# One section for the four column-group products of a modulation step, and one tile for its weights

## The chip, the core and the metric

The program runs on one NeuronCore of a Trainium2 chip. The metric is the device time of one execution in microseconds. TensorE (PE; its weight loads are shown as PEld) multiplies, VectorE (DVE), ScalarE (ACT) and GpSimd (POOL) work element by element, and SyncE (SP) issues the transfers between HBM and the core's SBUF. Products land in PSUM, eight banks of 512 f32 a partition.

## What is computed

Two networks run one after the other over 256 tokens of width 1024. The first is a hybrid block (attention, a delta rule, an MLP) and a recurrent block with an MLP. The second is a two-layer block of a diffusion kind, whose every normalisation is shifted, scaled and gated by a modulation vector that depends on two conditioning vectors only, `c` and `c_ctx`:

```python
def modulation(cvec, w_mod, b_mod):
    m = jax.nn.silu(cvec) @ w_mod + b_mod
    return jnp.split(m[:, None, :], N_MOD, axis=-1)
...
ml = modulation(c, w_mod[i], b_mod[i])
mc = modulation(c_ctx[None, :], w_mod[i], b_mod[i])
hl = modulate(rmsnorm(xl, g_pre_mix[i]), ml[0], ml[1])
```

`w_mod[i]` is 1024 x 6144 f32, 25 MB a layer. As it depends on nothing else, this product may be made at any time before the second network needs it.

## The kernel before

The large products of the kernel are f32 split in two: each weight half is copied by ScalarE to a rounded part (`wh`, line 404) and VectorE takes the rest (`wl`, line 405), six of each in rotation (`NW = 6`); three raw halves (`wr`, `NR = 3`) are loaded ahead by SyncE (line 386). Three matmuls, high by high, high by low and low by high, make one product. They go through the helper at line 343, as all matmuls do; transposes go through line 367.

The modulation is different: plain f32, in 48 steps. A step is one of 2 layers, one of 3 pairs of the six vectors, and one of 8 slices of the inner dimension. Its stationary operand is 32 columns wide (`cs_t`, both conditioning vectors and zeros), and its 2048 output columns are four groups of 512, which land in the partitions 0 to 31, 32 to 63, 64 to 95 and 96 to 127 of one PSUM bank, `pm`. So a step is four matmuls on four different column groups of the array (lines 772 to 774), and eight steps accumulate into the bank before VectorE takes it out (line 780).

The weights of a step are 1 MB. `mod_load` (line 726) loads them as two tiles of 512 KB (`wm`, four buffers), products 0 and 1 from the first and 2 and 3 from the second. SyncE issues them from the same queue as the weights of the large products. The generator `mods` keeps two steps loaded ahead.

The program is put in order by a planner that takes instructions by priority as they become ready. The generator is advanced by `fill(n)` from many places: 18 steps woven into the delta rule of the first network, the others between MLP units and at the borders of stages. Each of the four matmuls stands under `tc.high_priority(-10)`, which puts it ten places later in priority than its place in the program, so each may be moved by itself behind other work of TensorE.

Of the kernel before, what the change touches and what calls it, by code (L numbers as in the profile page):

```python
# [10 lines left out]
F32 = mybir.dt.float32  # L11
# [4 lines left out]
P = 128  # L16
# [15 lines left out]
def _unit(w, k0, nk, cols):  # L32

    n = w.shape[1]
    a = w.reshape(-1, P, n)[k0 : k0 + nk][:, :, cols]
    return a.transpose(1, 0, 2).reshape(P, -1)
# [83 lines left out]
def _ncols(c):  # L120
    return c.stop - c.start if isinstance(c, slice) else len(c)
# [5 lines left out]
def _cols(t):  # L127

    parts, at = [], 0

    def add(name, a):
        nonlocal at
        a = a.reshape(P, -1)
        COLS[name] = (at, a.shape[1])
        at += a.shape[1]
        parts.append(a)

    def vec(v):
        return v.reshape(-1, P).T

    def taps(w):
        return w.reshape(w.shape[0], -1, P).transpose(2, 1, 0)

    add("hyb_conv", taps(t("hyb_conv_w")[0]))
    add("norm_w", vec(t("hyb_norm_w")[0]))
    add("rec_conv", taps(t("rec_conv_w")[0]))
    add("rec_conv_b", vec(t("rec_conv_b")[0]))
    add("rec_b_a", vec(t("rec_b_a")[0]))
    add("rec_b_x", vec(t("rec_b_x")[0]))
    add("lam", vec(t("rec_lambda")[0]))  # L150
    for i in range(2):
        add(f"g_q{i}", vec(t("g_q_2")[i]))
        add(f"g_kv{i}", vec(t("g_kv_2")[i]))
        add(f"conf_w{i}", taps(t("conf_dw_w_2")[i]))
        add(f"conf_b{i}", vec(t("conf_dw_b_2")[i]))
        add(f"sc_w{i}", taps(t("sc_dw_w_2")[i]))
    return np.concatenate(parts, axis=1)
# [5 lines left out]
def _rows(t):  # L163
    r = []
    for i in range(2):
        for a in (1, 2):
            for b in "gb":
                r.append(t(f"ln{a}_{b}")[i])
    for i in range(2):
        r.append(t("g_branch_2")[i])  # L170
    for i in range(2):
        r.append(np.concatenate([t("conf_ln_g_2")[i], t("conf_ln_b_2")[i], np.zeros(512, np.float32)]))
    r.append(
        np.concatenate(
            [t("hyb_sinks")[0][HEAD_ORDER], t("hyb_a_log")[0], t("hyb_dt_bias")[0], np.zeros(1008, np.float32)]
        )
    )
    return np.stack(r)
# [50 lines left out]
def _pack(inputs):  # L229
    def t(name):  # L230
        return np.asarray(inputs[name])

    units = _weight_units(t)
    sizes = [(nk * _ncols(c), nk) for _, _, nk, c in units]
    wp = np.zeros((len(units), P, 2048), np.float32)
    for n, un in enumerate(units):
        a = _unit(*un)
        wp[n, :, : a.shape[1]] = a
    wm = np.ascontiguousarray(
        t("w_mod_2").reshape(2, 8, P, 3, 2, 1024).transpose(0, 3, 1, 4, 2, 5)  # L240
    )
    one = np.ones(1024, np.float32)
    bg = []
    for i in range(2):
        b = t("b_mod_2")[i].reshape(12, 512)
        g = np.concatenate(
            [one, t("g_pre_mix_2")[i], t("g_post_mix_2")[i], one, t("g_pre_mlp_2")[i], t("g_post_mlp_2")[i]]
        ).reshape(12, 512)
        bg.append(np.stack([b, g], 1).reshape(3, 4, 1024))
    cc = np.zeros((P, 8, 32), np.float32)  # L250
    cc[:, :, 0] = t("c_2")[0].reshape(8, P).T
    cc[:, :, 1] = t("c_ctx_2").reshape(8, P).T
    x = t("x")[0]
    kc0, kc1 = _consts()
    arrays = {
        "x": np.ascontiguousarray(x.reshape(2, P, 1024)),
        "xT": np.ascontiguousarray(x.T.reshape(8, P, 256).transpose(1, 0, 2)),
        "ctx": np.ascontiguousarray(t("ctx_2")[0].reshape(2, P, 1024)),
        "wp": wp,
        "wm": wm,  # L260
        "bg": np.ascontiguousarray(np.stack(bg)),
        "cc": cc,
        "cols": np.ascontiguousarray(_cols(t)),
        "rows": _rows(t),
        "kc": kc0,
        "kch": kc1,
    }
    return arrays, sizes
# [26 lines left out]
def hybrid_then_mla(ctx: ExitStack, tc: tile.TileContext, a, out, usizes):  # L295
    nc = tc.nc
    V, S, G, T = nc.vector, nc.scalar, nc.gpsimd, nc.tensor
    cpool = ctx.enter_context(tc.tile_pool(name="cpool", bufs=1))
    wpool = ctx.enter_context(tc.tile_pool(name="wpool", bufs=1))
# [8 lines left out]
    def nm(s):  # L308
        uid[0] += 1
        return f"{s}_{uid[0]}"  # L310
# [4 lines left out]
    def s4(shape, dt=F32):  # L315
        return tmp.tile(shape, dt, tag="s4", bufs=5, name=nm("s4"))

    def s2(shape, dt=F32):
        return tmp.tile(shape, dt, tag="s2", bufs=9, name=nm("s2"))
# [13 lines left out]
    def psC():  # L333
        return psp.tile([P, 512], F32, tag="pc", bufs=1, name=nm("pc"))

    def psM():
        return psp.tile([P, 512], F32, tag="pm", bufs=1, name=nm("pm"))
# [4 lines left out]
    def mm(o, l, r, start, stop):  # L342
        T.matmul(o, l, r, start=start, stop=stop)  # L343
# [12 lines left out]
    def K(name):  # L356
        w, o, n = KC[name]
        return kcs[w][:, o : o + n]
# [7 lines left out]
    def tr(o, i):  # L366
        T.transpose(o, i, ident)  # L367
# [345 lines left out]
    cs_t = cpool.tile([P, 8, 32], F32, name="cs_t")  # L713
# [9 lines left out]
    class WM:  # L723
        tiles, n = {}, 0

    def mod_load():

        if WM.n >= 48:
            return
        i, q, k = WM.n // 24, WM.n // 8 % 3, WM.n % 8  # L730
        for j in range(2):
            wm = wpool.tile([P, 2, 512], F32, tag="wm", bufs=4, name=nm("wm"))
            if WM.n < 2:
                G.tensor_copy(wm[:, 0, 0:1], WM.after)
            nc.sync.dma_start(out=wm, in_=a["wm"][i, q, k, j].rearrange("p (a b) -> p a b", a=2))
            WM.tiles[WM.n, j] = wm
        WM.n += 1

    mc = cpool.tile([P, 2, 3, 32], F32, name="mc")
# [7 lines left out]
    def mods():  # L747

        def cols_of(m, i, q):
            pt = psC()  # L750
            for c in range(4):
                tr(pt[:, 128 * c : 128 * c + 128], m[:, 128 * c : 128 * c + 128])
            V.tensor_copy(mc[:, i, q].rearrange("p (c r s) -> p c r s", c=4, r=4),
                          pt.rearrange("p (c r s) -> p c r s", c=4, r=4)[:, :, :, 0:2])

        todo = None
        for n in range(48):
            i, q, k = n // 24, n // 8 % 3, n % 8
            if k == 0:
                ps = psM()  # L760
            if k == 1 and todo:
                cols_of(*todo)
            if k == 4:
                bg = s4([P, 2, 512])
                for r in range(4):
                    nc.sync.dma_start(
                        out=bg[32 * r : 32 * r + 32],
                        in_=a["bg"][i, q, r : r + 1].rearrange("o (a b) -> o a b", a=2).to_broadcast([32, 2, 512]),
                    )
            while WM.n < min(n + 2, 48):  # L770
                mod_load()
            for r in range(4):
                with tc.high_priority(-10):
                    mm(ps[32 * r : 32 * r + 32, :], cs_t[:, k, :], WM.tiles[n, r // 2][:, r % 2, :], k == 0, k == 7)
            mod_load()
            if k < 7:
                yield
                continue
            m = s2([P, 512])
            V.tensor_tensor(m, ps, bg[:, 0, :], op=ADD)  # L780
            V.scalar_tensor_tensor(m, m, K("one")[:, q : q + 1], bg[:, 1, :], op0=ADD, op1=MUL)
            for r in range(4):
                if 2 * q + r // 2 in (2, 5):
                    nc.sync.dma_start(
                        out=mdr[i, :, 2 * q + r // 2, 512 * (r % 2) : 512 * (r % 2) + 512], in_=m[32 * r : 32 * r + 2]
                    )
            todo = (m, i, q)
            yield
        cols_of(*todo)
        yield  # L790

    mod_g = mods()

    def fill(n):
# [1268 lines left out]
```

## Time and profile before

| | |
|---|---|
| median of three runs | 1644.76 us (1640.21 to 1647.02) |
| the profiled execution, whole | 1647.52 us |
| span of its profile | 1645.5 us |
| TensorE busy | 1592.7 us, 97% |
| VectorE, ScalarE, GpSimd busy | 1032.0, 745.0, 95.6 us |
| transfers | 259.80 MB, 47.8% of 16 DMA engines' span |

Times in the rows are microseconds from the start of the span. "Busy" is the union of an engine's instructions; matmuls overlap, and the ends of their records are modelled. The chain that ended last is followed back from the last instruction, at each step to what released it.

### The profile page before, as it was taken

The page shows a single profiled execution, that of the slowest core. Times are in us where ns is not written, and L with a number is a line of the kernel's source. Part 1 is how long each engine was busy: PE and PEld are TensorE (multiplying, and loading weights), DVE is VectorE, ACT ScalarE, POOL GpSimd, SP SyncE. Part 2 cuts the span into 40 slices and gives each one's busy share as a digit, 9 for nine tenths or more (in the row PEclk, how much of TensorE's full clock was granted, in tenths as well). Part 3 has the DMA queues.
Part 4 walks back from the last instruction along what each step waited for, and adds up shares of the span by engine and source line. Part 5 has one row for each costly group of instructions (what it writes and reads, how often), then busy time and mean ns, then how long its engine had stood idle before and what let it go on. Part 6 is the DMA issues. An engine that isn't in the chain of part 4 may idle for free.

```text
span 1645.5 us, 25334 instructions
## 1 busy us (share of the span) xinstructions
PE 1592.7 (97%) x10182; PEld 1363.7 (83%) x10182; DVE 1032.0 (63%) x1593; ACT 745.0 (45%) x1264; POOL 95.6 (6%) x121
## 2 busy tenths in 40 slices
PE   8989999999989999998999999999999999989998
PEld 7856688887878998986877889999999878779997
DVE  6875475556787556777974753444444879765554
ACT  5642244443574445436344543322222565454443
POOL 0012000000000000003010100000000120000000
PEclk9999999999999999999999999999999999989999
DMA  8765576665658655443330343223223353146553
GB/s 281 254 235 187 180 225 221 207 199 180 212 181 291 209 192 175 165 166 103 118 101 26 129 141 103 90 90 103 92 88 103 118 184 96 58 133 204 181 192 103
DMA packets 72869, 259.80 MB, mean 158 GB/s; under 512 B 8480, under 2 KB 8736, under 8 KB 72752
## 3 DMA queue, kind: packets, MB, share of 16 engines
q1 hardware_dynamic: 72752, 258.19, 47.8%
q8 instruction: 80, 1.31, 0.3%
q14 instruction: 37, 0.30, 0.1%
HBM read 257.08 MB, written 1.08 MB: 157 GB/s over the span
## 4 chain that ended last, share of the span: by engine, by line
PE 81%; DVE 7%; ACT 3%; POOL 1%; issue 1%; DMA 1%; POOLq 0%; DVEq 0%; ACTq 0%; SPq 0%
PE pa L343 45%; PE pb L343 27%; PE pm L343 5%; PE pb L367 3%; DVE wl L405 1%; PE pc L367 1%; ACT s L1385 1%; POOL ti L1391 1%; DMA wr<-in_wp_dram 1%; DVE s L1579 1%; ACT wh L404 1%; DVE s L643 0%; DVE s L1404 0%; DVE b L709 0%; DVE b L647 0%
## 5 line engine op out<-in xcount | busy, mean ns | idle before, releaser
L405 DVE TENSOR_TENSOR wl<-wr,wh 128x1024 fp32r<-128x1024 f32 (+2 forms) x366 | 444.1, 1218 | 313.3 <-ACT wh L404 300.0
L404 ACT CAST wh<-wr 128x1024 fp32r<-128x1024 f32 (+2 forms) x364 | 377.2, 1042 | 451.2 <-PE pa L343 200.2
L343 PE MATMUL pa<-wh,b 128*128 128x512 f32 (+3 forms) x1456 | 409.9, 363 | 11.1 <-ACT b L646 5.6
L343 PE MATMUL pb<-b,wh 128*128 128x256 f32 x2240 | 406.6, 284 | 0.0
L343 PEld LDWEIGHTS pb<-b,wh 128*128 128x128 f32 x2240 | 352.8, 192 | 8.0 <-issue 3.4
L343 PE MATMUL pb<-b,wl 128*128 128x256 f32 x1120 | 317.7, 284 | 0.0
L343 PEld LDWEIGHTS pa<-wh,b 128*128 128x128 f32 x1456 | 266.1, 194 | 57.8 <-ACT b L646 6.1
L343 PE MATMUL pa<-wl,b 128*128 128x512 f32 (+3 forms) x728 | 257.2, 362 | 1.1 <-DVE wl L405 1.1
L343 PE MATMUL pa<-wh,s 128*128 128x512 f32 x768 | 244.5, 391 | 0.0
L343 PEld LDWEIGHTS pb<-b,wl 128*128 128x128 f32 x1120 | 215.0, 192 | 3.4 <-issue 3.4
L343 PE MATMUL pa<-b,wh 128*128 128x256 f32 x1056 | 198.7, 289 | 1.1 <-ACT b L646 0.8
L343 PEld LDWEIGHTS pa<-b,wh 128*128 128x128 f32 x1056 | 166.6, 193 | 14.2 <-issue 4.2
L343 PEld LDWEIGHTS pa<-wh,s 128*128 128x128 f32 x768 | 144.3, 188 | 29.3 <-DVE s L453 0.3
L343 PEld LDWEIGHTS pa<-wl,b 128*128 128x128 f32 x728 | 141.7, 195 | 24.6 <-issue 5.0
L343 PE MATMUL pa<-b,wl 128*128 128x256 f32 x528 | 149.9, 286 | 0.8 <-DVE wl L405 0.8
L343 PE MATMUL pa<-wl,s 128*128 128x512 f32 x384 | 150.1, 391 | 0.0
L343 PEld LDWEIGHTS pa<-b,wl 128*128 128x128 f32 x528 | 101.8, 193 | 2.9 <-issue 1.9
L343 PE MATMUL pm<-wm,cs_t 128*32 128x512 f32 x384 | 96.5, 618 | 4.7 <-DMA wm<-in_wm_dram 4.7
L343 PEld LDWEIGHTS pa<-wl,s 128*128 128x128 f32 x384 | 72.3, 188 | 13.4
L558 DVE TENSOR_TENSOR s<-s 128x512 f32<-128x512 f32 x80 | 54.9, 686 | 42.2 <-ACT s L556 42.2
L367 PE MATMUL pb<-kc_sb,s 128*128 128x128 f32 x366 | 59.9, 288 | 13.2 <-POOL s L1482 6.4
L1579 DVE SCALAR_TENSOR_TENSOR s<-cu,cols_sb,s 128x512 f32<-128x512 f32 (+1 forms) x120 | 71.7, 628 | 0.3
(278 smaller groups left out, 1405.8 us busy)
## 6 DMA issues: line engine op xcount, KB each, us to landing
wr<-in_wp_dram SPq DMA_DIRECT2D x354, 512.0 KB, 4.4
wm<-in_wm_dram SPq DMA_DIRECT2D x96, 512.0 KB, 4.7
row<-in_rows_dram SPq DMA_DIRECT2D x10, 512.0 KB, 5.4
wr<-in_wp_dram SPq DMA_DIRECT2D x8, 416.0 KB, 4.8
s<-in_bg_dram SPq DMA_DIRECT2D x24, 128.0 KB, 7.0
row<-mdr SPq DMA_DIRECT2D x6, 512.0 KB, 4.5
wr<-in_wp_dram SPq DMA_DIRECT2D x4, 264.0 KB, 3.7
b<-in_xT_dram SPq DMA_DIRECT2D x4, 256.0 KB, 4.2
```

The costliest lines, as they stand in the source:

```text
L343: T.matmul(o, l, r, start=start, stop=stop)
L367: T.transpose(o, i, ident)
L404: S.copy(h[:, :n], r)
L405: V.tensor_tensor(l[:, :n], r, f(h[:, :n]), op=SUB)
L558: V.tensor_tensor(q, r, r, op=MUL)
L1385: S.activation(j, x, AF.Square, scale=scale, accum_out=o)
L1391: G.tensor_tensor(r, e, half[:, :1], op=POW)
L1579: V.scalar_tensor_tensor(ac, src, w(k), ac, op0=MUL, op1=ADD)
```

## The change

The four matmuls of a step are put into one `tc.tile_critical()` section, under one `tc.high_priority(-10)`: one unit to the planner, between whose instructions nothing else is placed. The two weight tiles of a step become one of 1 MB, two buffers in place of four of half the size, loaded by one transfer; the array in HBM is laid out anew to suit, so that a partition's 2048 numbers lie together. Everything else, the six split halves among it, stays.

```diff
     wm = np.ascontiguousarray(
-        t("w_mod_2").reshape(2, 8, P, 3, 2, 1024).transpose(0, 3, 1, 4, 2, 5)
+        t("w_mod_2").reshape(2, 8, P, 3, 4, 512).transpose(0, 3, 1, 2, 4, 5)
     )
@@ mod_load
         i, q, k = WM.n // 24, WM.n // 8 % 3, WM.n % 8
-        for j in range(2):
-            wm = wpool.tile([P, 2, 512], F32, tag="wm", bufs=4, name=nm("wm"))
-            if WM.n < 2:
-                G.tensor_copy(wm[:, 0, 0:1], WM.after)
-            nc.sync.dma_start(out=wm, in_=a["wm"][i, q, k, j].rearrange("p (a b) -> p a b", a=2))
-            WM.tiles[WM.n, j] = wm
+        wm = wpool.tile([P, 4, 512], F32, tag="wm", bufs=2, name=nm("wm"))
+        if WM.n < 2:
+            G.tensor_copy(wm[:, 0, 0:1], WM.after)
+        nc.sync.dma_start(out=wm, in_=a["wm"][i, q, k])
+        WM.tiles[WM.n] = wm
         WM.n += 1
@@ mods
-            for r in range(4):
-                with tc.high_priority(-10):
-                    mm(ps[32 * r : 32 * r + 32, :], cs_t[:, k, :], WM.tiles[n, r // 2][:, r % 2, :], k == 0, k == 7)
+            with tc.high_priority(-10), tc.tile_critical():
+                for r in range(4):
+                    mm(ps[32 * r : 32 * r + 32, :], cs_t[:, k, :], WM.tiles[n][:, r, :], k == 0, k == 7)
             mod_load()
```

## Rows read from the trace of the kernel before

**Rows 1.** The page: busy time and chain that ended last.

```profile
PE 1592.7 (97%) x10182; PEld 1363.7 (83%) x10182; DVE 1032.0 (63%) x1593; ACT 745.0 (45%) x1264; POOL 95.6 (6%) x121
...
PE 81%; DVE 7%; ACT 3%; POOL 1%; issue 1%; DMA 1%; POOLq 0%; DVEq 0%; ACTq 0%; SPq 0%
PE pa L343 45%; PE pb L343 27%; PE pm L343 5%; PE pb L367 3%; DVE wl L405 1%; PE pc L367 1%; ACT s L1385 1%; POOL ti L1391 1%; DMA wr<-in_wp_dram 1%; DVE s L1579 1%; ACT wh L404 1%; DVE s L643 0%; DVE s L1404 0%; DVE b L709 0%; DVE b L647 0%
```

**Rows 2.** Stretches: length, busy time of each engine, granted clock, DMA share, GB/s.

```profile
82.00:200.00 118.00, 112.51 (x700) 70.98 (x699) 68.41 (x118) 38.94 (x117) 21.09 (x17) 1.00 0.60 202
200.00:405.00 205.00, 205.00 (x1255) 174.92 (x1254) 120.97 (x153) 87.65 (x104) 2.91 (x3) 1.00 0.64 208
...
1300.00:1370.00 70.00, 65.79 (x409) 52.99 (x410) 58.68 (x117) 48.48 (x102) 16.46 (x24) 0.95 0.53 177
```

**Rows 3.** Waits of TensorE: us in total, times, longest.

```profile
PE pb L367 <- POOL s L1482: 6.4, 2, 4.1
...
PE pm L343 <- DMA wm<-in_wm_dram: 4.7, 1, 4.7
...
PE pb L367 <- DVE s L1404: 2.0, 6, 0.6
```

**Rows 4.** The tile pm: its records (ns, shortest, median, longest); busy time of its group.

```profile
L343 PE MATMUL pm<-wm,cs_t x384: 592/593/1063, 82.9 to 1366.4; 128*32 128x512 f32 x192
...
L343 PE MATMUL pm<-wm,cs_t 128*32 128x512 f32 x384 | 96.5, 618 | 4.7 <-DMA wm<-in_wm_dram 4.7
```

**Rows 5.** Timeline of TensorE: pieces of pm, first and last among them.

```profile
82.89 1.05 PE L343 MATMUL pm<-wm,cs_t 128*32 128x512 f32 x2
...
1356.29 1.07 PE L343 MATMUL pm<-wm,cs_t 128*32 128x512 f32 x8
...
1365.92 1.06 PE L343 MATMUL pm<-wm,cs_t 128*32 128x512 f32 x6
```

**Rows 6.** The page's transfers: issuer, count, KB each, median us from issue to landing.

```profile
wr<-in_wp_dram SPq DMA_DIRECT2D x354, 512.0 KB, 4.4
wm<-in_wm_dram SPq DMA_DIRECT2D x96, 512.0 KB, 4.7
...
wr<-in_wp_dram SPq DMA_DIRECT2D x4, 264.0 KB, 3.7
```

**Rows 7.** Timeline of SyncE ahead of the first and the last step.

```profile
79.10 4.27 SPq L386 DMA_DIRECT2D wr<-in_wp_dram  x3
...
1349.64 4.75 SPq L386 DMA_DIRECT2D wr<-in_wp_dram  x3
```

**Rows 8.** Waits, all engines: weight loads for pm that waited for nothing shown.

```profile
PEld pm L343 <- issue: 15.2, 49, 0.8
```

**Rows 9.** Timeline of TensorE: three stops, in brackets how long, and by whom ended.

```profile
456.37 1.91 PE L343 MATMUL pm<-wm,cs_t 128*32 128x512 f32 x2 [4.71 <-DMA wm<-in_wm_dram]
...
754.72 0.45 PE L367 MATMUL pb<-kc_sb,s 128*96 128x128 f32 x1 [4.07 <-POOL s L1482]
...
1411.04 1.15 PE L343 MATMUL pa<-b,b 96*128 96x256 f32 x4 [2.08 <-ACT s L1648]
```

**Rows 10.** Stretches around these stops; the granted clock is third from last.

```profile
446.00:456.20 10.20, 5.53 (x43) 3.67 (x41) 10.20 (x19) 9.47 (x21) 0.00 (x0) 1.00 0.71 218
456.40:459.60 3.20, 3.20 (x8) 1.54 (x9) 3.20 (x4) 1.21 (x3) 0.00 (x0) 0.50 1.02 413
...
754.80:760.00 5.20, 5.20 (x17) 1.98 (x18) 4.33 (x9) 3.81 (x8) 3.25 (x7) 0.50 0.69 219
1411.10:1418.80 7.70, 6.92 (x35) 5.90 (x36) 5.30 (x16) 4.19 (x13) 1.25 (x2) 0.56 0.00 1
```

**Rows 11.** Waits of SyncE's queue: us in total, times, longest.

```profile
SPq L386 <- DVE wl L405: 1044.8, 325, 20.8
SPq L735 <- PE pm L343: 157.3, 48, 12.6
```

## The prediction

> **What bounds the kernel now.** I read the page first, then the stretches, then the waits of TensorE, then the tile pm by itself. On the page TensorE is busy for 97% of the span, and 81% of the chain that ended last runs over it; the group "PE pm L343" alone holds 5% of that chain, about 82 us [rows 1]. The table of stretches says the same of every stage: TensorE is busy for 112.5 of 118 us even in the stage where it is not alone, and VectorE is nowhere above 84% [rows 2]. So a microsecond of TensorE time is a microsecond of the kernel's nearly everywhere, and this holds for time saved and for time lost. The waits of TensorE are few: the longest sum is 6.4 us, and it waited only once for modulation weights, for 4.7 us [rows 3].
>
> **What a modulation step costs now.** A step is four products that write four groups of 32 partitions of one bank. Each product has two records (f32 operands are passed twice), so a step is eight records and 48 steps are 384. The view of the tile pm shows 592 ns as the shortest and 593 ns as the median record [rows 4]. The timeline shows what makes them dear or cheap: a piece of two records alone takes 1.05 us, a piece of six takes 1.06 us, and a whole step of eight takes 1.07 us [rows 5]. Products of different groups overlap almost entirely; the price is per uninterrupted piece, not per product. With other work between them each piece pays its own microsecond. Reading the records of the trace in order I count 94 pieces for the 48 steps, the first and the last of which stand in [rows 5]; a piece ends where other work of TensorE comes in, or where the same group comes round again.
>
> **Removed: the split.** One piece a step leaves 48 of 94, so 46 pieces go. From the start of a lone piece to the start of the next work is 0.98 us (82 us of the chain and 96.5 us of the tile's busy time [rows 1, 4] are of that size). 46 x 0.98 = 45 us. The check by busy time gives 96.5 - 48 x 1.07 = 45 us. As TensorE is the bound I count it in full, also between 82 and 200 us.
>
> **Added: the section's borders.** As I read the construct, a section is one unit for the scheduler and not merely an order of four products: its body is a block of its own, which TensorE enters behind a wait for what the schedule has put before it on all queues, transfers included, and leaves with a drain. The diff doesn't spell these instructions out and the trace has none, so both are bounded.
>
> Entry: no row prices it directly, but the trace shows what was under way when a step began. SyncE issued 354 weight transfers, which took 4.4 us to land, and 96 modulation transfers, which took 4.7 us [rows 6]; 354 x 4.4 + 96 x 4.7 is 2009 us of landing in a span of 1645 us, so more than one is under way on average. At the start of 38 of the 48 steps a transfer had been issued less than 4.6 us before. The first step starts at 82.89 us, behind three weight loads from 79.10 us on; the last starts at 1356.8 us, inside the piece at 1356.29 us, behind three issued from 1349.64 us on, the last of them at about 1354 us [rows 5, 7]. Summed over the 48, the rest until landing (or until the end of the instruction that VectorE or ScalarE had running, where that is later) is 108 us, 2.25 us a step. Today nobody waits for this rest: these loads fill buffers for work that comes later. From below the price is nearly nothing, if the order of the schedule puts the loads behind the section; from above it is 140 us, if the 1 MB loads of the new tile and the splits that the schedule has placed earlier count too. I take 85 us, the 108 less a fifth, because where two steps lie close together the second finds less under way, and because the 4.7 us that were waited for are in it already.
>
> Exit: the nearest rows are the times for which weight loads for pm stood with nothing but the sequencer to wait for, 15.2 us in 49 times, 0.31 us each, and the short waits of transposes for VectorE, 2.0 us in 6 times [rows 8, 3]. From 0.1 to 0.5 us a section; I take 0.31 us, 48 x 0.31 = 15 us.
>
> Clock: a stop costs more than itself. After the 4.71 us stop at 456.4 us the granted clock was 0.50 (1.2 GHz) for the next 3.2 us, where it had been 1.00 (2.4 GHz) before; after the 4.07 us stop at 754.7 us it was 0.50 for 5.2 us, and after 2.08 us of stop at 1411 us it averaged 0.56 over 7.7 us [rows 9, 10]. Half rate for 3.2 to 7 us loses 1.6 to 3.5 us. Thirty of the 48 rests above are longer than 1.2 us. If every one of them lost 2 us it would be 60 us; but not every stop in the trace was followed by half rate, and stops close together share a stretch, so I take 30 us, from 0 to 60. The Trainium skill (TensorE: Matmul & The Clock Gate, "Loop structure matters more than you think") warns that a wait in front of each burst of matmuls leaves them at the lower clock; these rows agree. Read strictly, all thirty would pay, and the sum would come out 30 us higher.
>
> **Moved: the weights.** 96 loads of 512 KB become 48 of 1 MB, in the same 16 KB a partition. SyncE already stood 157.3 us in 48 waits for room in wm [rows 11], and weight loads are queued behind it. A half came free after two products and now only the whole section frees it, so the wait grows by up to the time between a step's pieces. I cost it at nothing: two steps are held in advance, and the weight loads behind it (325 waits, 1044.8 us [rows 11]) arrive early today. If that cover is gone, a late weight load stops TensorE for up to a landing, 4.4 us. Products 0 and 1 now wait for products 2 and 3's weights too; one such wait of 4.7 us exists today. POOL's four tiny copies become two, long before their use. The number of split halves stays six.
>
> **The sum.** 1647.5 us is the profiled execution's own time (span 1645.5 us), 0.2% over the median of the three runs, 1644.8 us. -45 + 85 + 15 + 30 = +85 us, so 1732 us by the profile and **1730 us** against the median. The ends of this case: -45 + 54 + 5 + 10 = +24 us (1670 us) with half of the entry waits, and -45 + 140 + 25 + 60 = +180 us (1825 us), to which I leave some room.
>
> **The rivals.**
> 1. The borders are light (**17%**): the section only orders, or what it waits for has landed. For it: TensorE waits little today, and 10 of the 48 starts had no transfer under way. Then the 45 us stand against 0 to 15 us of exits: 1600 to 1617 us, likeliest 1605 us. It decides where entry and exit together stay below 45 / 48 = 0.94 us a section. Against it: the 2.25 us that are under way at a mean start.
> 2. Both sides balance, or the split stays as it is because something else cuts the step (**6%**): 1637 to 1653 us.
> 3. Entering and leaving costs a fetch of code (**7%**): two jumps a section, 96 in all. Nothing in this trace jumps; the nearest row is a transfer's landing, from 3.7 us upward [rows 6]. If half of the 96 stood for 3.7 us each, that is 178 us more than the light case, 1780 us, and with the entry waits 1870 us or over. The Trainium skill (Runtime: NRT & Kernel Launch, "Instruction fetch mechanics") says that a taken branch to code outside the fetched window stalls for such a fetch; no row here shows one.
>
> **How the numbers follow.** My forecast, the entry waits decide, has **70%**, 1665 to 1850 us. A half per cent, 8 us, is about what a measurement of this kernel can tell from no change. Slower by more: forecast and rival 3, 77%. Within it: rival 2, 6%. Faster: rival 1, 17%. The range 1610 to 1850 us holds the forecast but for 2%, rival 2 and half of rival 1: about 82%. The likeliest case alone is 1665 to 1850 us.
>
> **What would show it.** Records of pm in 48 pieces of eight, the tile's busy time near 50 us instead of 96.5 us: the gain is real. Idle time before pm, some 2 us in most of 48 cases, ended by transfers of wr or by ScalarE and VectorE, none of which pm reads: the entry wait. Further stretches of half clock right behind these stops. About 0.3 us of idle after each pm piece: the exit. TensorE's busy share would fall from 97% to near 90%. The prediction is wrong if pm's idle time stays near 5 us while its busy time halves (rival 1), or if the idle time sits ahead of each piece with no transfer or engine that ends it (rival 3).

## The result, and the profile after

The changed kernel takes **1769.4 us** (median of four runs, 1765.3 to 1770.8) against 1645.4 us beside it: ratio **1.0756, 95% interval 1.0724 to 1.0787**. That is 124 us more, where 85 us were forecast, inside the range. The profiled execution took 1768.1 us, with a span of 1766.2 us.

The page of the changed kernel, the lines that answer to [rows 1]:

```profile
PE 1590.8 (90%) x10182; PEld 1377.7 (78%) x10182; DVE 1028.7 (58%) x1593; ACT 744.7 (42%) x1264; POOL 95.8 (5%) x119
...
PEclk9979899999888999998899999999999999989999
...
q8 instruction: 82, 1.34, 0.3%
...
PE 14%; DVE 1%; ACT 1%; DMA 0%; issue 0%; POOL 0%; DVEq 0%; POOLq 0%; ACTq 0%
```

TensorE is busy for 1591 us, as before, in a span that is 121 us longer; its share fell from 97% to 90%. The chain as followed back covers only some 16% of the span here, where it covered nearly all of it in [rows 1], so it is not used below.

The groups of pm in the changed kernel (busy, mean ns | idle before), then the records of the tile (ns, shortest, median, longest), for [rows 4] and [rows 8]:

```profile
L343 PE MATMUL pm<-wm,cs_t 128*32 128x512 f32 x384 | 69.0, 793 | 118.5 <-DMA wm<-in_wm_dram 27.3 <-DMA wr<-in_wp_dram 21.4 <-issue 8.5
...
L343 PEld LDWEIGHTS pm<-wm,cs_t 128*32 128x32 f32 x384 | 8.8, 120 | 139.8 <-issue 139.7
```

```profile
L343 PE MATMUL pm<-wm,cs_t x384: 592/617/1063, 89.1 to 1477.5; 128*32 128x512 f32 x192
```

The 48 steps now stand in 48 pieces, and the idle time in front of them has grown from 4.7 to 118.5 us. What ended it, from the waits of TensorE and of SyncE's queue (us in total, times, longest), for [rows 3] and [rows 11]:

```profile
PE pm L343 <- DMA wm<-in_wm_dram: 27.3, 6, 5.8
PE pm L343 <- DMA wr<-in_wp_dram: 21.4, 8, 5.9
PE pm L343 <- issue: 8.5, 3, 5.4
PE pm L343 <- DVE xt L658: 7.2, 2, 4.9
...
PE pm L343 <- POOL ti L1390: 5.5, 1, 5.5
```

```profile
SPq L734 <- PEq L771: 291.4, 46, 17.4
```

No product of pm reads raw halves `wr`, `xt` or `ti`. These are waits of the border, not of the data. The single names are not to be taken at their word, though: the profile puts a wait for several semaphores (the counters by which engines and transfers tell that they are done) down to the one that came last. The trace holds what the section really stood on. Each of the 48 sections is entered through the same seven instructions of TensorE, and these name thirteen semaphores: eight that transfers raise, two of TensorE, and one each of VectorE, ScalarE and GpSimd. Matched with the times at which these rose, the 118.5 us are 46.3 us of waiting for the next step's weights to land, 30.3 us for raw halves, 9.8 us for other transfers and engines, and 32.1 us of the border's own instructions. The 5.5 us put down to `ti`, for one, were a wait for the next step's weights.

Places in the timeline of TensorE in the changed kernel (start, duration, in brackets the idle before and what ended it), and the stretches around the last of them (length, busy time, then clock, DMA share, GB/s):

```profile
190.00 1.06 PE L343 MATMUL pm<-wm,cs_t 128*32 128x512 f32 x8 [0.43 <-issue]
...
514.67 1.94 PE L343 MATMUL pm<-wm,cs_t 128*32 128x512 f32 x8 [3.85 <-ACT b L1338]
522.52 1.94 PE L343 MATMUL pm<-wm,cs_t 128*32 128x512 f32 x8 [5.91 <-DMA wr<-in_wp_dram]
524.67 1.19 PE L343 MATMUL pa<-b,wh 128*128 128x256 f32 x4 [0.22 <-PEq L771]
...
801.12 1.93 PE L343 MATMUL pm<-wm,cs_t 128*32 128x512 f32 x8 [5.37 <-issue]
...
804.57 1.93 PE L343 MATMUL pm<-wm,cs_t 128*32 128x512 f32 x8 [0.48 <-PE pb L367]
```

```profile
780.00:795.70 15.70, 15.54 (x120) 14.74 (x118) 15.11 (x29) 9.14 (x18) 2.24 (x4) 1.00 0.27 79
...
801.10:804.60 3.50, 2.41 (x13) 0.41 (x13) 0.00 (x0) 0.00 (x0) 0.00 (x0) 0.50 0.20 30
804.60:808.00 3.40, 3.18 (x13) 1.15 (x14) 0.62 (x2) 0.00 (x0) 0.00 (x0) 0.50 0.66 277
```

At 190 us no transfer was under way: the border cost 0.43 us and the step 1.06 us. At 514 and 522 us two sections follow each other, and the second waits for 5.91 us. Behind it 0.22 us go by until the next matmul. At 801 us the stop is followed by two stretches at clock 0.50 (1.2 GHz), where it was 1.00 (2.4 GHz) ahead of it. A step takes 1.93 us there instead of 1.06 us.

SyncE's queue in the timeline, and the page's row of these loads (count, KB, median us to landing), show what had been issued ahead of the section at 522.52 us; the last line, from the view of the tile `wr` between 515 and 524 us, is the landing of the one raw half issued there, at 517.24 us:

```profile
516.81 0.33 SPq L734 DMA_DIRECT2D wm<-in_wm_dram  x1
517.24 0.37 SPq L386 DMA_DIRECT2D wr<-in_wp_dram  x1
```

```profile
wm<-in_wm_dram SPq DMA_DIRECT2D x48, 1024.0 KB, 4.8
```

```profile
DMA to landing us min/median/max: 5.6/5.6/5.6
```

The section before it ended at 516.6 us and so freed a buffer. The load for the step after next was issued into it at once and landed 4.8 us later, at 521.6 us; 0.9 us after that, the section began. It has its own weights since long before; it waited for its successor's. The raw half that the row names landed at 522.8 us, after the section had begun, so the section did not wait for it. Nor is this the only one: at 19 of the 48 starts a transfer that had been issued was still under way, and six times it was the very load that the section before had released. This fits a wait for what the planner has placed before the section, and not for all that is under way; the planner's order itself is not in the trace.

**The account.** I summed the records of both traces by kind:

| us, from the trace | before | after | difference |
|---|---|---|---|
| TensorE busy with pm | 96.5 | 69.0 | -27.5 |
| TensorE busy with the rest | 1496.1 | 1521.8 | +25.7 |
| idle before pm | 4.7 | 118.5 | +113.8 |
| idle elsewhere | 48.1 | 56.9 | +8.8 |
| span | 1645.5 | 1766.2 | +120.7 |

At full clock 48 whole steps would be 48 x 1.07 = 51 us; so fewer pieces gave back 45 us of pm, and half clock took 18 us of it again. With the 25.7 us on other work, whose matmuls are the same, the clock cost some 44 us. A second reading agrees: within the span, stretches at clock 0.50 add up to 168 us, 120.2 us of them with TensorE busy, where they were 42 and 35.1 us before; half of the 85 us more is 43 us.

### The profile page after: what moved, and what is told of

Its sections match the earlier page's. It is cut to its first block, busy times and chain, and to the rows that moved or that the text cites. A ratio compares the mean times of both kernels' runs of the same rounds, so it can differ in the third digit from the quotient of the medians.

```text
span 1766.2 us, 25841 instructions
## 1 busy us (share of the span) xinstructions
PE 1590.8 (90%) x10182; PEld 1377.7 (78%) x10182; DVE 1028.7 (58%) x1593; ACT 744.7 (42%) x1264; POOL 95.8 (5%) x119
## 5 line engine op out<-in xcount | busy, mean ns | idle before, releaser
L404 ACT CAST wh<-wr 128x1024 fp32r<-128x1024 f32 (+2 forms) x364 | 377.3, 1041 | 469.9 <-PE pa L343 224.7
L343 PE MATMUL pa<-wh,b 128*128 128x512 f32 (+3 forms) x1456 | 414.4, 366 | 13.1 <-ACT b L646 5.8
L343 PE MATMUL pa<-b,wh 128*128 128x256 f32 x1056 | 204.9, 294 | 4.9 <-ACT wh L404 1.4
L343 PEld LDWEIGHTS pa<-b,wh 128*128 128x128 f32 x1056 | 171.7, 199 | 16.8 <-issue 10.1
L343 PE MATMUL pm<-wm,cs_t 128*32 128x512 f32 x384 | 69.0, 793 | 118.5 <-DMA wm<-in_wm_dram 27.3
L343 PEld LDWEIGHTS pm<-wm,cs_t 128*32 128x32 f32 x384 | 8.8, 120 | 139.8 <-issue 139.7
```

Source lines behind the costliest of these rows:

```text
L404: S.copy(h[:, :n], r)
```

## The experiments

Four sets ran; the kernel before had medians of 1645.4, 1642.0, 1643.3 and 1642.9 us in them. Diffs are against the changed kernel. "Idle" is TensorE's idle time before pm, "busy" its time with pm, both of the profiled execution.

| kernel | us | ratio to before (95%) | idle | busy |
|---|---|---|---|---|
| changed | 1769.4 | 1.0756 (1.0724 to 1.0787) | 118.5 | 69.0 |
| e1_tile_only | 1630.2 | 0.9935 (0.9909 to 0.9960) | 0.0 | 87.1 |
| e2_section_only | 1749.8 | 1.0649 (1.0624 to 1.0674) | 105.9 | 69.0 |
| e3_no_border | 1637.7 | 0.9973 (0.9953 to 0.9992) | 9.2 | 50.1 |
| e4_border_only | 1851.2 | 1.1272 (1.1242 to 1.1301) | 141.7 | 143.1 |
| e5_loads_in_pairs | 1764.8 | 1.0744 (1.0726 to 1.0762) | 117.2 | 69.8 |
| e6_half_sections | 1683.2 | 1.0247 (1.0229 to 1.0265) | 53.6 | 64.8 |
| e7_two_sections | 1914.4 | 1.1659 (1.1629 to 1.1689) | 169.2 | 149.4 |
| e8_top_first18 | 1623.3 | 0.9882 (0.9864 to 0.9899) | 0.5 | 76.6 |
| e9_short_load | 1754.5 | 1.0674 (1.0650 to 1.0698) | 98.8 | 70.1 |
| e10_short_load_free | 1637.8 | 0.9965 (0.9952 to 0.9978) | 5.4 | 92.1 |
| e11_pair_sections | 1670.2 | 1.0166 (1.0142 to 1.0191) | 44.6 | 59.1 |

### The two parts one by one

**e1_tile_only**: the single tile, the four products as before.

```diff
-            with tc.high_priority(-10), tc.tile_critical():
-                for r in range(4):
+            for r in range(4):
+                with tc.high_priority(-10):
                     mm(ps[32 * r : 32 * r + 32, :], cs_t[:, k, :], WM.tiles[n][:, r, :], k == 0, k == 7)
```

> The weights of a step as one tile of 1 MB, without the section: the four products are again placed one by one. If the section's borders cost the 124 us, this one stands near the kernel before, 1630 to 1650 us, with idle time before pm near 5 us as in [rows 4]. If the single tile costs them (room that comes free later, SyncE held up in front of the weight loads), it is slow without any section, 1720 us or more, and TensorE waits for wr or wm.

**e2_section_only**: the section, with the two tiles of before.

```diff
-        wm = wpool.tile([P, 4, 512], F32, tag="wm", bufs=2, name=nm("wm"))
...
+        for j in range(2):
+            wm = wpool.tile([P, 2, 512], F32, tag="wm", bufs=4, name=nm("wm"))
...
-                    mm(ps[32 * r : 32 * r + 32, :], cs_t[:, k, :], WM.tiles[n][:, r, :], k == 0, k == 7)
+                    mm(ps[32 * r : 32 * r + 32, :], cs_t[:, k, :], WM.tiles[n, r // 2][:, r % 2, :], k == 0, k == 7)
```

> The section with the weights in two tiles of 512 KB as before. If the borders cost the time, it stays where the changed kernel is, 1755 to 1785 us, with about 118 us of idle time before pm. If the single tile is to blame, it takes about 1600 us: 45 us less than before for the unsplit pieces.

The groups of pm, of e1_tile_only and of e2_section_only:

```profile
L343 PE MATMUL pm<-wm,cs_t 128*32 128x512 f32 x384 | 87.1, 628 | 0.0
```

```profile
L343 PE MATMUL pm<-wm,cs_t 128*32 128x512 f32 x384 | 69.0, 793 | 105.9 <-DMA wr<-in_wp_dram 36.8 <-DMA wm<-in_wm_dram 20.0 <-ACT s L1385 6.7
```

The tile alone comes out 0.65% under the kernel before: nothing waits for pm's weights any more, and the steps happen to fall into 84 pieces, not 94. The section alone brings 108 us, and its time is 5 us under the range expected. So the loss is the section's. But the two don't just add: with the section, the one tile costs 20 us more than the two (1769.4 against 1749.8 us).

### The gain without the border

**e3_no_border**: no section, but the step's four products at top priority, which keeps 43 runs of whole steps together.

```diff
-            with tc.high_priority(-10), tc.tile_critical():
+            with tc.high_priority():
```

> The single tile, no section, and the four products at the highest priority, so that the planner places them next to each other: 48 steps in 43 uninterrupted runs, no border. If the gain of the unsplit step is real and only the borders eat it, 1590 to 1610 us (1645 less 45), with the busy time of pm near 50 us, idle time before it near 5 us, and a granted clock of 0.98. If the unsplit step is worth nothing because other work fills TensorE anyway, 1640 to 1650 us.

The page's group of pm in e3_no_border:

```profile
L343 PE MATMUL pm<-wm,cs_t 128*32 128x512 f32 x384 | 50.1, 603 | 9.2 <-DMA wm<-in_wm_dram 8.7 <-DVE s L779 0.5
```

A miss. The busy time of pm fell by 46.4 us, just as the pieces say, but the kernel gained only 4.3 us. Against the trace of before, the other work's busy time grew by 10.7 us and idle time by 26.7 us. At top priority the steps also move forward: six of them start in the first 80 us instead of none, and in the two stages from 426 to 1007 us (439 to 1004 us before) idle time is 34 us instead of 17. So this kernel changed two things, whole steps and their places, and the 45 us are probably gone in part because a step that is early fills no later hole. That part is argued, not shown.

**e8_top_first18**: top priority only for the 18 steps of the first stage, the others free to be split, no section.

```diff
-            with tc.high_priority(-10), tc.tile_critical():
-                for r in range(4):
+            for r in range(4):
+                with tc.high_priority() if n < 18 else tc.high_priority(-10):
                     mm(ps[32 * r : 32 * r + 32, :], cs_t[:, k, :], WM.tiles[n][:, r, :], k == 0, k == 7)
```

> The single tile without a section; the 18 steps of the first network at the highest priority (unsplit there), the other 30 as before. If unsplit steps save where TensorE is the bound, and the loss of the kernel without borders came from moving the later steps, this takes 1618 to 1630 us, below the single tile alone (1630 us). If split pieces cost little because they fill gaps of TensorE in the first network, 1630 to 1640 us.

This is the fastest kernel of the study, 1.2% under the kernel before and inside the range expected: pm is busy for 20 us less than before and idle time before it is 0.5 us. The later steps stay free to be split. Of the 20 us that the kernel gains, 12 us come with the single tile alone (e1); against that kernel pm is busy for 10.5 us less, and the time is 7 us less.

### What a border costs

**e4_border_only**: only the first of the four products stands in the section.

```diff
             with tc.high_priority(-10), tc.tile_critical():
-                for r in range(4):
+                mm(ps[0:32, :], cs_t[:, k, :], WM.tiles[n][:, 0, :], k == 0, k == 7)
+            for r in range(1, 4):
+                with tc.high_priority(-10):
                     mm(ps[32 * r : 32 * r + 32, :], cs_t[:, k, :], WM.tiles[n][:, r, :], k == 0, k == 7)
```

> The section holds the first product of each step alone; the other three are placed one by one. 48 borders, and the steps are still split into some 75 pieces. If a border costs what it seems to, whatever it encloses, this takes the changed kernel's time and about 25 us for the 27 more pieces: 1780 to 1810 us. If the long unsplit unit itself is what stalls (four products held back together until all is there), it comes out well below the changed kernel, 1700 us or less.

The timeline of TensorE in e4_border_only:

```profile
111.32 1.04 PE L343 MATMUL pm<-wm,cs_t 128*32 128x512 f32 x2 [1.53 <-POOL s L1006]
112.71 1.06 PE L343 MATMUL pm<-wm,cs_t 128*32 128x512 f32 x6 [0.34 <-PEq L771]
...
121.76 1.91 PE L343 MATMUL pm<-wm,cs_t 128*32 128x512 f32 x2 [4.18 <-issue]
124.02 1.93 PE L343 MATMUL pm<-wm,cs_t 128*32 128x512 f32 x6 [0.34 <-PEq L771]
```

More than expected, for a reason that the rows show. The border also stands behind the section: 0.34 us lie between the lone product and the other three, so they don't overlap, and a step costs two pieces even where nothing else comes between. Of the 87 us over the changed kernel's span, 74 us are pm's busy time and 23 us idle before it, with 10 us less elsewhere. Of the 74 us, some 50 us are the second piece of each step (48 x 1.05); the rest is half clock, as in the second pair of rows. One product in a section waits no less than four do.

**e6_half_sections**: sections for the odd steps alone; the even ones at top priority.

```diff
-            with tc.high_priority(-10), tc.tile_critical():
+            with tc.high_priority(-10) if n % 2 else tc.high_priority(), tc.tile_critical() if n % 2 else ExitStack():
```

> Sections for the 24 odd steps alone; the 24 even steps stand unsplit without a border (highest priority, as in the kernel without borders, which took 1637.7 us). If each border pays by itself, the time lies halfway between 1637.7 and 1769 us: 1690 to 1715 us, with 50 to 65 us of idle time before pm. If what costs is a chain of sections one behind the other (each waits for the last), well under that, 1660 us or less.

**e7_two_sections**: two sections a step, 96 in all.

```diff
-            with tc.high_priority(-10), tc.tile_critical():
-                for r in range(4):
-                    mm(ps[32 * r : 32 * r + 32, :], cs_t[:, k, :], WM.tiles[n][:, r, :], k == 0, k == 7)
+            for h in range(2):
+                with tc.high_priority(-10), tc.tile_critical():
+                    for r in (2 * h, 2 * h + 1):
+                        mm(ps[32 * r : 32 * r + 32, :], cs_t[:, k, :], WM.tiles[n][:, r, :], k == 0, k == 7)
```

> Two sections a step, products 0 and 1 and products 2 and 3: 96 borders. The second follows the first closely and finds little new under way. If the entry pays for what is under way, the second costs its code and its piece only, 48 x (0.7 + 0.3 + 1.0) = 96 us with little more idle time than 40 us before pm: 1850 to 1885 us. If every border costs the mean of the changed kernel, 2.5 us of idle time and the clock, 48 x (2.5 + 0.3 + 1.0) = 182 us and more: 1940 us or over.

**e11_pair_sections**: one section for two steps, 24 in all.

```diff
-            with tc.high_priority(-10), tc.tile_critical():
-                for r in range(4):
-                    mm(ps[32 * r : 32 * r + 32, :], cs_t[:, k, :], WM.tiles[n][:, r, :], k == 0, k == 7)
-            mod_load()
+            if n % 2:
+                with tc.high_priority(-10), tc.tile_critical():
+                    for k2 in (k - 1, k):
+                        for r in range(4):
+                            mm(ps[32 * r : 32 * r + 32, :], cs_t[:, k2, :], WM.tiles[n - k + k2][:, r, :], k2 == 0, k2 == 7)
+                mod_load()
+                mod_load()
```

> Two steps in one section: 24 borders for the same 48 steps and eight products behind each; both next loads follow it. Theory, the price is one of the border and not of the products: half of 118.5 us idle before pm, of 9 us behind it and of the clock's 44 us go, some 85 us, so 1680 to 1700 us, near the 1683 us of the kernel in which every other step has a section. Rival: with 2 MB of loads released at once each border waits longer and the saving is lost: above 1720 us.

The group of pm in e11_pair_sections, and one of its sections in the timeline of TensorE:

```profile
L343 PE MATMUL pm<-wm,cs_t 128*32 128x512 f32 x384 | 59.1, 744 | 44.6 <-issue 9.2 <-ACT wh L404 5.8 <-DVE b L1606 3.9
```

```profile
167.28 1.92 PE L343 MATMUL pm<-wm,cs_t 128*32 128x512 f32 x16 [0.43 <-ACT s L1011]
```

Idle before pm a border: 1.86 us with 24 (e11), 2.47 us with 48, 1.76 us with 96 (e7). The price does not go with the products behind a border: e11 has the same 384 records and came out 99 us below the changed kernel, under the 1680 to 1700 us expected. With the 24 borders went 74 us of idle time before pm and much of the slow stretches (62 us at clock 0.50, not 168). But the number of borders alone doesn't set it either. By the semaphores (table at the end of the next section), 17 us of the 74 us are the code of the borders that are gone, and 46 us are waits for the next step's weights, which no section of e11 has. e6 came out 7 us under its range; half of its steps also changed place, so it is the weaker of the two. e7 added 145 us: 51 us of idle before pm, 1.06 us for each further border, of which 44 us are code and only 7 us waits; and 80 us of busy time of pm, some 50 us of it because the two halves of a step no longer overlap (96 x 1.05 us in place of 48 x 1.07 us), the other 30 us at the lower clock. The rest is other work at the lower clock. Its time lies between the two theories' ranges, and both of these terms are why.

### What the border waits for

**e5_loads_in_pairs**: both next loads issued behind every odd step.

```diff
-            while WM.n < min(n + 2, 48):
+            while WM.n < min(n + 1 + (n == 0), 48):
...
-            mod_load()
+            if n % 2:
+                mod_load()
+                mod_load()
```

> The changed kernel, but the loads of the two next steps are both issued behind the odd step of a pair, none between its two sections. If an entry waits for what is under way whether or not the section reads it, the second sections of the five pairs that now stand 5.4 to 5.9 us until the load just issued has landed fall to about 1.4 us: 22 us less, some 10 us less at half clock, 1735 to 1750 us. If a border has a fixed price, no change: 1760 to 1775 us.

The two close sections of above in e5_loads_in_pairs, in the timeline of all engines:

```profile
510.78 1.94 PE L343 MATMUL pm<-wm,cs_t 128*32 128x512 f32 x8 [3.98 <-DVE s L1308]
...
512.91 0.33 SPq L734 DMA_DIRECT2D wm<-in_wm_dram  x1
...
518.55 1.94 PE L343 MATMUL pm<-wm,cs_t 128*32 128x512 f32 x8 [5.84 <-DMA wr<-in_wp_dram]
```

The expected gain did not come, and the run doesn't speak on the theory: the load still stands between the two sections. The planner places it as soon as its buffer is free, whatever its place in the program, and the sections and weight loads stand in the same order on SyncE as in the changed kernel. So the next pair of runs changed the load's size.

**e9_short_load** and **e10_short_load_free**: from the third step on a quarter of the columns, into the tile that is there; with the sections, and without.

```diff
+        if WM.n < 2:
             wm = wpool.tile([P, 4, 512], F32, tag="wm", bufs=2, name=nm("wm"))
...
+        else:
+            wm = WM.tiles[WM.n % 2]
+            nc.sync.dma_start(out=wm[:, :, 0:128], in_=a["wm"][i, q, k][:, :, 0:128])
```

> The changed kernel (48 sections, one tile a step), but from the third step on only a quarter of the columns is loaded, into the tile that the step before last has left: 256 KB in place of 1 MB, at the same places; its modulation is computed from old weights for the rest. Theory: a border waits for whatever is under way, its own successor's weights too, which it does not need; the five longest stops in front of pm (5.5 to 5.9 us, 28.4 us in sum) are each the second of two sections close together, waiting for the load that the first one released. A quarter of the bytes should land in 2 to 3 us in place of 4.8, so each of these stops loses 2 to 2.5 us and the lesser ones some of it: idle before pm 118.5 -> 90 to 105 us, the time 1740 to 1757 us. Rival: the stops are other engines' work and the code of the border, and the load merely ends last among several: idle before pm above 112 us, the time 1762 to 1770 us.

> The control: the same shortened loads in the kernel without sections (one tile a step, four separate products at -10), which leaves out the same part of the computation. If the bytes matter to nothing but the borders, it stands within 0.4% of 1630 us, the time of that kernel with whole loads (1624 to 1637). If the 35 MB less of traffic speed up the other transfers as well, it is faster by as much as the sectioned one: 1605 to 1622 us.

Two close sections in the timeline of TensorE of e9_short_load, and its loads on the page (count, KB, us to landing):

```profile
463.99 1.07 PE L343 MATMUL pm<-wm,cs_t 128*32 128x512 f32 x8 [0.43 <-issue]
468.74 1.22 PE L343 MATMUL pm<-wm,cs_t 128*32 128x512 f32 x8 [3.69 <-DMA wm<-in_wm_dram]
```

```profile
wm<-in_wm_dram SPq DMA_DIRECT2D x46, 256.0 KB, 3.0
```

The first section begins after 0.43 us, the second waits for the load that the first released. The five longest stops of the changed kernel (steps 27, 29, 37, 41 and 43, counted from 0) can be followed by their step through three sizes of that load. In all fifteen the wait ends with the landing of the next step's weights:

| load that the section waits for | its landing there | the five stops | sum |
|---|---|---|---|
| 1 MB (changed) | 4.8 to 5.0 us | 5.9, 5.8, 5.5, 5.7, 5.5 | 28.4 |
| the first of two of 512 KB (e2) | 3.4 to 3.8 us | 4.1, 4.9, 4.2, 4.4, 4.5 | 22.1 |
| 256 KB (e9) | 2.9 to 3.1 us | 3.7, 4.1, 3.5, 3.6, 3.6 | 18.5 |

In e2_section_only a section releases two loads, and the next one waits for the first alone. SyncE's queue and the section of step 27 there:

```profile
502.98 0.33 SPq L735 DMA_DIRECT2D wm<-in_wm_dram  x1
...
503.82 6.04 SPq L735 DMA_DIRECT2D wm<-in_wm_dram  x3
```

```profile
506.93 1.94 PE L343 MATMUL pm<-wm,cs_t 128*32 128x512 f32 x8 [4.14 <-DVE s L1341]
```

The first half landed at 506.4 us, and the section began 0.6 us later; the second half, issued at 503.82 us, landed only at 509.2 us. In e9_short_load the planner has also moved steps: 27 and 29 stand at 468.7 and 510.4 us, not at 522.5 and 566.5 us. Steps 37, 41 and 43 stand where they stood, and show the same.

The kernel with the short load is 15 us faster than the changed one (1754.5 us, inside the 1740 to 1757 us expected), while without sections the short load is 8 us slower than the whole one (1637.8 against 1630.2 us, a little over the range; its steps fall into 91 pieces, not 84). So fewer bytes gain nothing where there is no border, and with borders a section waits for a load that it doesn't need. For these transfers an experiment shows it. For raw halves and engines the semaphores show it, without an experiment of their own. The idle time before pm by what ended the wait, in us:

| kernel | sections | next step's weights | raw halves | other | code of the border |
|---|---|---|---|---|---|
| changed | 48 | 46.3 | 30.3 | 9.8 | 32.1 |
| e2_section_only | 48 | 32.6 | 29.9 | 11.5 | 31.8 |
| e9_short_load | 48 | 32.1 | 26.5 | 9.6 | 30.6 |
| e11_pair_sections | 24 | 0.0 | 23.3 | 6.3 | 15.0 |
| e7_two_sections | 96 | 58.4 | 26.5 | 8.5 | 75.8 |

## Why the prediction was right, point by point

**The direction and the mechanism held**: the entry of the section decides, and what it waits for are transfers and engines that pm doesn't read. The terms, forecast against measured:

| term | forecast | measured | from |
|---|---|---|---|
| split removed | -45 | -45 | 96.5 less 48 x 1.07 |
| entry | +85 (54 to 140) | +114 | idle before pm: waits 86, code 32, less the 5 of before |
| exit | +15 (5 to 25) | +9 | idle elsewhere |
| clock | +30 (0 to 60) | +44 | pm +18, the rest +26 |
| sum | +85 | +121 | spans |

**Entry, too small by 29 us, for a term that was left out.** The waits themselves came to 86 us, 82 us more than before, where I took 85 us for them; that they fit so closely is in part luck. I took off a fifth because the second of two close sections should find less under way. It is the reverse where it waits for the load that the first released: five such sections hold the longest stops, 28.4 us together. And I named raw halves, ScalarE and VectorE as what would end the waits. They and a few other transfers ended 40 us of them; the other 46 us ended with the next step's weights, which stood only in my upper bound. What I priced at nothing is the code of the border itself, 32 us. The rows of the line on which the sections' waits stand in the changed kernel (count, ns shortest, median, longest):

```profile
L2058 PEldq EVENT_SEMAPHORE  x290: 51/51/6577, 82.1 to 1766.1; - x145
L2058 PEldq COMPARE_BRANCH  x48: 163/163/303, 88.8 to 1476.8; - x48
```

These are six waits a section, in the trace about 106 ns from one to the next, and a branch with 0.22 us from its start to the first matmul: 6 x 0.106 + 0.22 is about 0.86 us. Often a part of it runs while TensorE still works or while the entry waits; what is left is 32.1 us over 48 sections, 0.67 us each.

**Exit, nearly right.** I had 0.31 us a section; 8.8 us over 48 is 0.18 us, and single rows show 0.22 and 0.34 us. Counted directly, 8.2 us of idle time lie right behind the 39 sections that other work follows.

**Clock, 14 us too small.** The cause was right, and the rows at 801 to 808 us show it as [rows 9, 10] did. The Trainium skill (TensorE: Matmul & The Clock Gate, "Loop structure matters more than you think") says that a long wait for a transfer between matmuls leaves them at the lower clock. The trace agrees: TensorE is busy for 120.2 us at clock 0.50 (1.2 GHz), where it was 35.1 us before. Read strictly, as I did for every rest above 1.2 us, it gave 60 us, and the 44 us lie midway between that and my 30.

**The gain, right as TensorE time, doubtful as kernel time.** I counted 45 us in full, as TensorE bounds the kernel nearly everywhere. The account has them. But e3_no_border shows that 46 us less of pm can come to 4 us of the kernel if the whole steps also move. The step of the prediction that fails there is "in full, also between 82 and 200 us": a step is work that fills holes as well as work that costs, and an unsplit one probably fills fewer of them. What whole steps would give in the same places without a border was not isolated; e8_top_first18 comes nearest, with 7 us of the kernel for 10.5 us of pm.

**The tile at nothing: right by itself, wrong beside the section.** e1_tile_only costs nothing, even gains 12 us. With the section, it costs 20 us (e2_section_only), mostly because the section behind then waits for 1 MB to land, where of two loads of 512 KB it waits for the first alone: 46.3 us of such waits in place of 32.6 us. I priced the two edits as if they were independent.

**The rivals.** Light borders: refuted by 118.5 us of idle time. A balance: refuted. A fetch of code: the page counts 82 packets of instructions, and before there were, on the page of the kernel before:

```profile
q8 instruction: 80, 1.31, 0.3%
```

The 48 sections have 48 branches (above), where the trace of before has none on TensorE. As many fetches more would show in this count, which is 84 even with the 96 sections of e7; and a border of 0.43 us contains no landing (the shortest median in these runs is 3.0 us). The Trainium skill (Runtime: NRT & Kernel Launch, "Instruction fetch mechanics") has such a stall for a branch out of the fetched window; no run here shows one.

## What to carry to other kernels

A section that keeps a few instructions together also makes its engine wait for other queues and engines, even for work that it doesn't read: here thirteen semaphores before each of 48 sections, and, as far as the rows tell, for whatever the planner has placed before it. Price it by what of that is under way at that moment plus its code (here 0.67 us on average, 0.86 us in full), and not by its contents. Fewer, larger sections cost less (24 in place of 48: 1670 against 1769 us), and a load released by one section can be the next one's stop. Where products only have to stand close, a priority does it without a border, but only for steps that needn't fill later holes (1623 us, against 1630 us with the single tile alone and 1643 us before).

## What the runs showed that was not expected

- Two sections close together: the second costs more than the first where it waits for the load that the first released (5.91 us after 3.85 us). It costs little where it doesn't, though the load is under way (0.48 us at 804.6 us, after 5.37 us; the load had been issued at 803.25 us).
- The name by which the profile ends a wait for several semaphores can be wrong: the 5.91 us were put down to a raw half that landed after the section had begun.
- 0.34 us of exit code between products on different column groups are enough to make one piece of 1.07 us into two of 1.04 and 1.06 us.
- A section with nothing to wait for still costs 0.43 us to enter, in waits and a branch that find everything done; right behind another section, 1.4 us (at 469.9 us).
